# One 512-column pass for both parts of the activations, and PSUM banks handed out in pairs

## The chip, the cores and the metric

The kernel runs on one core of one Trainium2 chip. The metric is the device time of one execution in microseconds (us), as the median of several executions. Engines are named as in the profile: PE is the matrix engine, PEld its weight loads, DVE the vector engine, ACT the activation engine, POOL the general engine, SP the engine that issues most DMA transfers. PSUM is the memory that PE writes its results to; the kernel divides it into eight banks of 512 fp32 columns. "Evacuating" a bank means that ACT or DVE reads the finished result out of it.

## What is computed

Two transformer-like blocks on 256 tokens of width 1024, in fp32. Cut to what matters here:

```
h = rms_norm(x);  q,k,v,rq,rk,rv,rg,ga,gr = split(h @ w_in)
merged = sigmoid(ga) * (att @ w_att_o) + sigmoid(gr) * (ret @ w_ret_o)      # gate, merge
x = x + merged @ w_out
h = rms_norm(x)
x = x + (silu(h @ w_gate) * (h @ w_up)) @ w_down                            # feed-forward
x = second_block(rms_norm(x)):  gated MLP and banded attention, @ w_out, then
x = x + sum over the chosen experts of  g * gelu(expert_u . h) * expert_v   # 16384 experts
```

The expert layer is computed densely: `peer_u` has 128 slices of 128 experts, whose scores for all 256 tokens go through gelu and are multiplied by a sparse matrix of weights, and a second layer multiplies by `peer_v`.

## The kernel before

**Products in two parts.** Every fp32 operand of a large product is split into a high part of type fp32r and a low part, the rest. A product is then three matmuls per k step of 128 rows (`mm3`, L108): weights' high part with activations' high part, high with low, and low with high. Weights are streamed: `unit` (L77) loads 128x1024 values with one SP DMA into `raw`, ACT copies them to `whi` (L95), and DVE subtracts to `wlo` (L96). Six pairs of `whi` and `wlo` are there until the expert layer, three in it.

**Stages.** `gemm_t` (L117) runs 8 k steps of 256 columns (all tokens) into half of one PSUM bank; `gemm_n` (L139) turns the operands round and fills two banks of 128 tokens x 512 columns. In order of time: the q, k, v products (`dests`, L268), attention and retention, gate (L327 to L335, 16 x `gemm_t`), merge (L337 to L350), w_out (L354), the feed-forward layer's gate and up products (L376, 22 values of f) and w_down (L412), block 2 (`block2`, L528) with five `gemm_n` or `gemm_t` groups, and the expert layer (`peer`, L717): 16 query products (L955), 128 slices of the first layer (L994), then the second layer (L1064). Between slices of the first layer the sparse weights are formed and combined (`combine`, L931).

**PSUM.** `mm_bank` (L102) hands out one bank of four in turn, `ax_bank` (L105) one of four others for small products, transposes and the second layer. Before a bank is written again, PE waits for the evacuation of what was in it four `mm_bank` calls ago. The second query and first-layer slices use `mm_bank` too: two slices of 256 columns fill a bank, and ACT puts 512 columns through gelu (L1009; from the time `combine` runs, L1006 and L1009).

**Order.** The order on each engine is set by a scheduler at build time: each engine works off its instructions in that order, and waits on counters of the other engines. `unit` is run 80 places ahead (`AHEAD`).

**Norms.** A norm's per-token factor is made late: column sums by PE (L188), a reciprocal square root by small DVE instructions (L160 to L173), a row form by ACT and PE (L198 to L201). In the feed-forward layer the factor `R` multiplies gate and up (L397 to L401). At the start of block 2 the factor `rd` (L542) scales the q product's evacuation (`qraw`, L557).

Of the kernel before, what the change touches and what calls it, by code (L numbers as in the profile page):

```python
# [7 lines left out]
F32 = mybir.dt.float32  # L8
F32R = mybir.dt.float32r
# [3 lines left out]
AF = mybir.ActivationFunctionType  # L13
OP = mybir.AluOpType
# [14 lines left out]
T = 256  # L29
# [3 lines left out]
KF = FF // 128  # L33
# [8 lines left out]


class Net:
# [36 lines left out]
    def unit_(self, src, n, pieces, engine, between):  # L81
# [18 lines left out]
        return hi, lo  # L100

    def mm_bank(self):  # L102
        return self.psum.tile([128, 512], F32, name="mm", bufs=4)

# [3 lines left out]
    def mm3(self, ps, left, right, first, last):  # L108
        mm = self.nc.tensor.matmul
        mm(ps, lhsT=left[0], rhs=right[0], start=first, stop=False)  # L110
        mm(ps, lhsT=left[0], rhs=right[1], start=False, stop=False)  # L111
        mm(ps, lhsT=left[1], rhs=right[0], start=False, stop=last)  # L112

    def acts(self, hl, k, ts=slice(0, T)):
# [94 lines left out]
    def new_acts(self, pool, K=8, tag="act", bufs=2):  # L209
        return (pool.tile([128, K, T], F32R, tag=tag + "h", name=tag + "h", bufs=bufs),  # L210
                pool.tile([128, K, T], F32R, tag=tag + "l", name=tag + "l", bufs=bufs))

# [22 lines left out]
    def block1(self, actp):  # L235
        nc, a, tc = self.nc, self.a, self.tc
        mult, add, sub = OP.mult, OP.add, OP.subtract
        with ExitStack():
# [6 lines left out]
            first = self.unit_(a["w_in_a"][0], 1024, 4, nc.gpsimd, load_x)  # L245
            h = self.new_acts(actp)
# [13 lines left out]
            with ExitStack() as s1:  # L260
# [42 lines left out]
                both = self.xbp.tile([128, 8, T], F32R, tag="xbh", name="att", bufs=1)  # L303
                att = both[:, 0:4], both[:, 4:8]
                probs = [self.att1_probs(p, tb, aq, ak, mask) for tb in range(2)]
# [21 lines left out]
                for i in range(16):  # L327
                    ps = self.mm_bank()[:, :T]
                    self.gemm_t(ps, a["w_in_a"][14 + i], h, 8)
                    nc.vector.tensor_tensor(out=gate[:, i], in0=ps, in1=R, op=mult)  # L330
                    if i == 2:
                        self.turn_ret(osb, ret)
                    if i % 4 == 3:
                        g4 = gate[:, i - 3:i + 1].rearrange("p a b -> p (a b)")
                        nc.scalar.activation(g4, g4, AF.Sigmoid)  # L335
                mer = self.new_acts(actp)
                for m in range(8):  # L337
                    if m % 2 == 0:
                        hi, lo = self.unit(a["w_att_o"][m // 2], 1024)
                    ps = self.mm_bank()  # L340
                    for k in range(4):
                        s = slice((m % 2 * 4 + k) * 128, (m % 2 * 4 + k) * 128 + 128)
                        self.mm3(ps[:, :T], (hi[:, s], lo[:, s]), self.acts(att, k), k == 0, k == 3)
                    self.gemm_t(ps[:, T:], a["w_ret_o"][m], ret, 8)
                    m1 = p2.tile([128, T], F32, name="m1")
                    m2 = p2.tile([128, T], F32, name="m2")
                    nc.vector.tensor_tensor(out=m1, in0=ps[:, :T], in1=gate[:, m], op=mult)
                    nc.vector.tensor_tensor(out=m2, in0=ps[:, T:], in1=gate[:, 8 + m], op=mult)
                    nc.vector.tensor_tensor(out=m1, in0=m1, in1=m2, op=add)
                    self.split(m1, mer[0][:, m], mer[1][:, m])  # L350
# [15 lines left out]
            with ExitStack() as s1:  # L366
# [9 lines left out]
                for f in range(KF):  # L376
                    ps = self.mm_bank()
                    if f == 0:
# [4 lines left out]
                        continue  # L383
                    self.gemm_t(ps[:, :T], a["w_gate"][f], h, 8)
                    if f == 2:
                        R = self.rows(r, "rb")
                    self.gemm_t(ps[:, T:], a["w_up"][f], h, 8)
                    early.append((ps.rearrange("p (a t) -> p a t", a=2), None))
                    if 5 <= f < 21:
# [4 lines left out]
                    for f0, (g, u) in enumerate(early, f + 1 - len(early)):  # L394
                        gu = p2.tile([128, 2, T], F32, name="gu")
                        if f0:
                            nc.vector.tensor_tensor(out=gu, in0=g, in1=R[:, None, :].to_broadcast([128, 2, T]),  # L397
                                                    op=mult)
                        else:
                            nc.vector.tensor_tensor(out=gu[:, 0], in0=g, in1=R, op=mult)  # L400
                            nc.vector.tensor_tensor(out=gu[:, 1], in0=u, in1=R, op=mult)  # L401
                        nc.scalar.activation(gu[:, 0], gu[:, 0], AF.Silu)
                        nc.vector.tensor_tensor(out=gu[:, 1], in0=gu[:, 0], in1=gu[:, 1], op=mult)
                        self.split(gu[:, 1], hid[0][:, f0], hid[1][:, f0])
                    early = []
# [311 lines left out]
    def peer(self, st, x3, h, acc):  # L717
        nc, a, tc = self.nc, self.a, self.tc
        mult, add, sub = OP.mult, OP.add, OP.subtract
        with tc.using_default_side("right"):  # L720
# [5 lines left out]
            pick = p.tile([128, 3, 128], F32, name="pick")  # L726
        xb = self.new_acts(self.xbp, tag="xb", bufs=1)
        hand = self.pool("hand", 2, st)
# [456 lines left out]
```

## Time and profile before

| | us |
|---|---|
| median of 3 runs | 1287.78 (1287.43 to 1288.07) |
| profiled execution | 1289.19, of which span 1287.4 |
| PE busy | 1276.2 (99%) |
| DVE busy | 904.6 (70%) |
| ACT busy | 718.7 (56%) |

The profile shows one execution. Its span runs from the first to the last instruction of the core; the rest of the execution's time, 1.8 us, lies around it. A matmul's end is modelled, so that neighbouring matmuls overlap in the rows: the time of a matmul in a stream is read from the distance of two starts.

### The profile page before, as it was taken

How to read it: one execution, taken by the hardware profiler on the slowest of the kernel's cores; microseconds unless marked ns; L12 is line 12 of the kernel's file. 1: busy time of each engine (PE TensorE's matmuls, PEld its weight loads, DVE VectorE, ACT ScalarE, POOL GpSimd, SP SyncE). 2: the span in 40 equal slices, each digit the busy share in tenths (PEclk: the TensorE clock that was granted, in tenths of full speed). 3: DMA queues.
4: the chain of work that ended last, by engine and by line, in shares of the span. 5: the costliest groups of instructions: out<-in, count | busy, mean ns of one | idle time of the engine just before them, and what ended most of it. 6: DMA issues, size and time to landing. Idle time of an engine off the chain costs nothing.

```text
span 1287.4 us, 23568 instructions
## 1 busy us (share of the span) xinstructions
PE 1276.2 (99%) x9125; PEld 1186.8 (92%) x9125; DVE 904.6 (70%) x1785; ACT 718.7 (56%) x1158; POOL 269.4 (21%) x173
## 2 busy tenths in 40 slices
PE   8999999999999999999999999999999999999998
PEld 7878999999999889999999999999988888888887
DVE  7767677766666886988895566776566666666665
ACT  5455545545455675655554676666555555555553
POOL 2000000000000000008778887773000000000000
PEclk9999999999999999999999999999999999999999
DMA  7745668965567544567777777776677777777764
GB/s 261 230 131 153 179 188 293 335 195 184 177 186 221 160 145 138 182 187 186 181 168 209 181 169 177 165 172 173 215 217 221 217 215 218 219 219 220 215 199 160
DMA packets 90928, 253.02 MB, mean 197 GB/s; under 512 B 26944, under 2 KB 28736, under 8 KB 90688
## 3 DMA queue, kind: packets, MB, share of 16 engines
q1 hardware_dynamic: 68816, 241.45, 61.0%
q0 software_dynamic: 20992, 8.46, 5.9%
q8 instruction: 71, 1.16, 0.4%
q10 hardware_dynamic: 1008, 1.61, 0.3%
q14 instruction: 41, 0.34, 0.1%
HBM read 240.93 MB, written 10.55 MB: 195 GB/s over the span
## 4 chain that ended last, share of the span: by engine, by line
PE 93%; DVE 5%; issue 1%; DMA 0%; ACT 0%; SPq 0%; ACTq 0%; DVEq 0%
PE ax L1069 27%; PE mm L110 21%; PE mm L112 20%; PE mm L111 20%; DVE wlo L96 2%; PE ax L942 1%; DVE itop L741 1%; PE ax L888 0%; DMA xT<-in_xT_dram 0%; DVE stop L739 0%; ACT whi L95 0%; DVE sc L744 0%; DVE pos L741 0%; PE ax L678 0%; PE ax L713 0%
## 5 line engine op out<-in xcount | busy, mean ns | idle before, releaser
L96 DVE TENSOR_TENSOR wlo<-raw,whi 128x1024 fp32r<-128x1024 f32 (+2 forms) x433 | 524.4, 1213 | 239.6 <-ACT whi L95 238.2
L95 ACT ACTIVATE whi<-raw 128x1024 fp32r<-128x1024 f32 (+3 forms) x439 | 457.9, 1045 | 313.2 <-PE mm L111 219.6
L110 PE MATMUL mm<-xbh,whi 128*128 128x256 f32 x1104 | 312.0, 283 | 0.0
L112 PE MATMUL mm<-xbh,wlo 128*128 128x256 f32 x1104 | 308.3, 279 | 0.3 <-DVE wlo L96 0.2
L111 PE MATMUL mm<-xbl,whi 128*128 128x256 f32 x1104 | 308.3, 279 | 0.2 <-DVE xbl L155 0.2
L832 POOL DMA_INDIRECT cmat<-best,pos x128 | 241.6, 1887 | 226.4 <-DVE itop L741 164.6
L110 PE MATMUL mm<-acth,whi 128*128 128x256 f32 x848 | 239.4, 282 | 3.0 <-DVE qkv L291 1.4
L111 PE MATMUL mm<-actl,whi 128*128 128x256 f32 x848 | 237.9, 281 | 1.5 <-DVE actl L253 1.5
L112 PE MATMUL mm<-acth,wlo 128*128 128x256 f32 x848 | 237.0, 280 | 0.0
L112 PEld LDWEIGHTS mm<-xbh,wlo 128*128 128x128 f32 x1104 | 207.4, 188 | 1.3 <-DVE wlo L96 0.9
L111 PEld LDWEIGHTS mm<-xbl,whi 128*128 128x128 f32 x1104 | 207.6, 188 | 0.4 <-DVE xbl L155 0.4
L110 PEld LDWEIGHTS mm<-xbh,whi 128*128 128x128 f32 x1104 | 207.6, 188 | 0.2 <-ACT xbh L154 0.2
L110 PEld LDWEIGHTS mm<-acth,whi 128*128 128x128 f32 x848 | 159.9, 189 | 4.3 <-DVE qkv L291 1.7
L111 PEld LDWEIGHTS mm<-actl,whi 128*128 128x128 f32 x848 | 160.1, 189 | 2.2 <-DVE actl L253 2.2
L112 PEld LDWEIGHTS mm<-acth,wlo 128*128 128x128 f32 x848 | 160.0, 189 | 0.2 <-DVE wlo L96 0.2
L1069 PE MATMUL ax<-whi,q 128*128 128x512 f32 x512 | 158.0, 389 | 0.0
L1069 PE MATMUL ax<-whi,keys 128*128 128x512 f32 x512 | 157.9, 389 | 0.0
L1069 PE MATMUL ax<-wlo,keys 128*128 128x512 f32 x512 | 157.9, 389 | 0.0
L154 ACT ACTIVATE keys<-S 128x256 fp32r<-128x256 f32 x128 | 53.5, 418 | 151.4 <-PE ax L1069 151.4
L1069 PEld LDWEIGHTS ax<-whi,q 128*128 128x128 f32 x512 | 96.1, 188 | 20.0
L1069 PEld LDWEIGHTS ax<-wlo,keys 128*128 128x128 f32 x512 | 96.1, 188 | 19.9
L1069 PEld LDWEIGHTS ax<-whi,keys 128*128 128x128 f32 x512 | 96.0, 188 | 20.0
(282 smaller groups left out, 1405.5 us busy)
## 6 DMA issues: line engine op xcount, KB each, us to landing
raw<-in_peer_u_dram SPq DMA_DIRECT2D x128, 512.0 KB
raw<-in_peer_v_dram SPq DMA_DIRECT2D x128, 512.0 KB
raw<-in_w_in_b_dram SPq DMA_DIRECT2D x32, 512.0 KB
raw<-in_w_in_a_dram SPq DMA_DIRECT2D x31, 512.0 KB
raw<-in_w_gate_dram SPq DMA_DIRECT2D x22, 512.0 KB
raw<-in_w_up_dram SPq DMA_DIRECT2D x22, 512.0 KB
raw<-in_w_out_dram SPq DMA_DIRECT2D x16, 512.0 KB
cmat<-zero SPq DMA_DIRECT2D x16, 512.0 KB
```

Of the source, the lines that this page charges most:

```text
L95: self.last_copy = nc.scalar.activation(hi[:, s], raw[:, s], AF.Copy).ins
L96: low = (engine or nc.vector).tensor_tensor(out=lo[:, s], in0=raw[:, s], in1=hi[:, s].bitcast(F32), op=OP.subtract)
L110: mm(ps, lhsT=left[0], rhs=right[0], start=first, stop=False)
L111: mm(ps, lhsT=left[0], rhs=right[1], start=False, stop=False)
L112: mm(ps, lhsT=left[1], rhs=right[0], start=False, stop=last)
L154: nc.scalar.activation(hi, src, AF.Copy)
L741: yield cost + 50, lambda: nc.vector.max_index(where[:, o:o + 8], top[:, o:o + 8], vals)
L832: i = nc.gpsimd.indirect_dma_start(self.cmat, bass.IndirectOffsetOnAxis(ap=ps[:, hd, 1, k:k + 1], axis=0), bs[:, hd, 1, k:k + 1], None, co ...
L942: nc.tensor.matmul(C[:, t * 128:t * 128 + 128], lhsT=A[:, t], rhs=G[i][:, t], start=i == 0, stop=i == 1)
L1069: nc.tensor.matmul(banks[tb][d], lhsT=s[left][:, ts], rhs=w[right][:, d * 512:d * 512 + 512], start=first, stop=end)
```

## The change

Where the weights are the stationary operand, the weights' high part meets both parts of the activations in one matmul of 512 columns: high and low part of one k lie side by side in one tile (`new_acts`), the result is high x high in columns 0 to 255 of a bank and high x low in 256 to 511, and the third matmul (low x high) adds to the first 256 columns (`mm2`). The two column halves are added behind it: ACT copies the second, DVE adds (`added`). This is done for gate, merge, the feed-forward gate and up products (f from 1 to 20) and w_down: 720 k steps. Query and expert products keep `mm3`.

PSUM is handed out anew: `mm_pair` is a tile of two banks with two buffers, in place of four single banks, and `mm_bank` gives the first and then the second bank of such a pair to every other product. `R` no longer multiplies the up product; it multiplies behind w_down.

```diff
-    def mm_bank(self):
-        return self.psum.tile([128, 512], F32, name="mm", bufs=4)
+    def mm_pair(self):
+        self.half = None
+        return self.psum.tile([128, 2, 512], F32, name="mm", bufs=2)
+
+    def mm_bank(self):
+        if self.half is None:
+            pair = self.mm_pair()
+            self.half = pair[:, 1]
+            return pair[:, 0]
+        bank, self.half = self.half, None
+        return bank
+    def mm2(self, ps, weight, acts, k, first, last):
+        mm = self.nc.tensor.matmul
+        both = acts[2][:, k]
+        mm(ps, lhsT=weight[0], rhs=both, start=first, stop=False)
+        mm(ps[:, :T], lhsT=weight[1], rhs=both[:, 0], start=False, stop=last)
+    def added(self, out, pair):
+        self.nc.scalar.activation(out, pair[:, :, T:], AF.Copy)
+        self.nc.vector.tensor_tensor(out=out, in0=pair[:, :, :T], in1=out, op=OP.add)
...
                 for i in range(16):
-                    ps = self.mm_bank()[:, :T]
-                    self.gemm_t(ps, a["w_in_a"][14 + i], h, 8)
-                    nc.vector.tensor_tensor(out=gate[:, i], in0=ps, in1=R, op=mult)
+                    if i % 2 == 0:
+                        pair = self.mm_pair()
+                    self.gemm_w(pair[:, i % 2], a["w_in_a"][14 + i], h, 8)
+                    if i % 2:
+                        two = gate[:, i - 1:i + 1]
+                        self.added(two, pair)
+                        nc.vector.tensor_tensor(out=two, in0=two, in1=R[:, None, :].to_broadcast([128, 2, T]),
+                                                op=mult)
...
                 for f in range(KF):
-                    ps = self.mm_bank()
+                    if 0 < f < KF - 1:
+                        pair = self.mm_pair()
+                        self.gemm_w(pair[:, 0], a["w_gate"][f], h, 8)
...
+                        self.gemm_w(pair[:, 1], a["w_up"][f], h, 8)
+                        gu = p2.tile([128, 2, T], F32, name="gu")
+                        self.added(gu, pair)
+                        early.append((gu[:, 0], gu[:, 1]))
+                    else:
+                        ps = self.mm_bank()
...
                 for m in range(8):
-                    ps = self.mm_bank()[:, :T]
+                    ps = self.mm_bank()
                     for j, (k0, K) in enumerate(((0, 8), (8, 8), (16, 6))):
-                        self.gemm_t(ps, a["w_down"][m, :, k0 * 128:(k0 + K) * 128], hid, K, k0, j == 0, j == 2)
-                    nc.vector.tensor_tensor(out=x2[:, m], in0=ps, in1=x1[:, m], op=add)
+                        self.gemm_w(ps, a["w_down"][m, :, k0 * 128:(k0 + K) * 128], hid, K, k0, j == 0, j == 2)
+                    y = p2.tile([128, T], F32, name="y")
+                    nc.scalar.activation(y, ps[:, T:], AF.Copy)
+                    nc.vector.tensor_tensor(out=y, in0=ps[:, :T], in1=y, op=add)
+                    nc.vector.tensor_tensor(out=y, in0=y, in1=R, op=mult)
+                    nc.vector.tensor_tensor(out=x2[:, m], in0=y, in1=x1[:, m], op=add)
```

The order of instructions moves at three places of which the next sections speak. Line numbers here are those of each kernel's own program: L130 to L132 after are `mm3` (L110 to L112 before), L106 and L107 are `whi` and `wlo` (L95, L96), L227 the column sums (L188), L238 the row form (L199), L610 the scaling of q (L557), L1063 the gelu (L1009). Words in brackets say on which engine's counter an instruction waits.

**PE in the first expert layer**, where one bank is full and the next begins. `mm_8557` and `mm_8632` are two banks of before:

```order
L110 MATMUL mm_8557<-xbh_5895,whi_8595 128x256
L111 MATMUL mm_8557<-xbl_5896,whi_8595 128x256
L112 MATMUL mm_8557<-xbh_5895,wlo_8596 128x256
L110 MATMUL mm_8632<-xbh_5895,whi_8634 128x256 [waits Activation_49]
L111 MATMUL mm_8632<-xbl_5896,whi_8634 128x256
L112 MATMUL mm_8632<-xbh_5895,wlo_8635 128x256 [waits DVE_49]
```

After, `mm_8246` is one pair: `whi_8329` belongs to the end of its first bank and `whi_8373` to the start of its second; `mm_8455` is the next pair.

```order
L132 MATMUL mm_8246<-xb_5230,wlo_8330 128x256
L130 MATMUL mm_8455<-xb_5229,whi_8457 128x256 [waits Activation_49]
L131 MATMUL mm_8455<-xb_5229,whi_8457 128x256
L130 MATMUL mm_8246<-xb_5229,whi_8373 128x256 [waits Activation_49]
L131 MATMUL mm_8246<-xb_5229,whi_8373 128x256
L132 MATMUL mm_8246<-xb_5229,wlo_8374 128x256 [waits DVE_49]
```

Two matmuls of the next pair now stand between the first and the second bank of one pair, and the second bank's first matmul carries a wait on ACT of its own, though its weights are two units older than those just used.

**ACT at the same place**, before and after:

```order
L95 ACTIVATE whi_8711<-raw_8710 128x1024 [waits DMAHW3_49,DVE_49,PE_49]
L1009 ACTIVATE S_6234<-mm_8557 128x512 [waits PE_49]
L95 ACTIVATE whi_8752<-raw_8751 128x1024 [waits DMAHW4_49,DVE_49,PE_49]
L95 ACTIVATE whi_8790<-raw_8789 128x1024 [waits DMAHW5_49,DVE_49,PE_49]
L1009 ACTIVATE S_6234<-mm_8632 128x512 [waits PE_49]
```

```order
L106 ACTIVATE whi_8403<-raw_8402 128x1024 [waits DMAHW4_49,DVE_49,PE_49]
L106 ACTIVATE whi_8457<-raw_8456 128x1024 [waits DMAHW5_49,DVE_49,PE_49]
L1063 ACTIVATE S_5565<-mm_8246 128x512 [waits PE_49]
L106 ACTIVATE whi_8487<-raw_8486 128x1024 [waits DMAHW6_49,DVE_49,PE_49]
L106 ACTIVATE whi_8543<-raw_8542 128x1024 [waits DMAHW7_49,DVE_49,PE_49]
L1063 ACTIVATE S_5565<-mm_8246 128x512 [waits PE_49]
```

ACT's order is the same in kind: one gelu of a bank behind every second weight copy, with one copy right ahead of it; both gelus of after read one pair. Counted along ACT's instructions, the counter value for which the first matmul with `whi_8373` waits is that of the first of these gelus.

**PE at the start of block 2.** The q product's two banks are `mm_4764` and `mm_4765` before, and the k product begins in `mm_4919`:

```order
L112 MATMUL mm_4765<-whi_4821,actl_4005 128x512
L188 MATMUL ax_4839<-ones_66,acc_4006 128x1 [waits DVE_49]
L188 MATMUL ax_4839<-ones_66,acc_4006 128x1
L188 MATMUL ax_4857<-ones_66,acg_4007 128x1 [waits DVE_49]
L188 MATMUL ax_4857<-ones_66,acg_4007 128x1
L110 MATMUL mm_4919<-whi_4922,acth_4004 128x512
```

After, q lies in the second bank of `mm_4026` (the first holds w_down's last column block) and in the first of `mm_4110`, and k begins in `mm_4264`, which has the buffer of `mm_4026`:

```order
L132 MATMUL mm_4110<-whi_4166,act_3499 128x512
L227 MATMUL ax_4184<-ones_66,acc_3500 128x1 [waits DVE_49]
L227 MATMUL ax_4184<-ones_66,acc_3500 128x1
L227 MATMUL ax_4202<-ones_66,acg_3501 128x1 [waits DVE_49]
L227 MATMUL ax_4202<-ones_66,acg_3501 128x1
L238 MATMUL ax_4439<-dg_4440,ones_66 128x128 [waits Activation_49]
L238 MATMUL ax_4439<-dg_4443,ones_66 128x128 [waits Activation_49]
L130 MATMUL mm_4264<-whi_4266,act_3499 128x512 [waits PE_49,Activation_49]
```

Of ACT's order after, what precedes and what releases that matmul:

```order
L237 ACTIVATE dg_4440<-ident_139,rcc_4183 128x128 [waits DVE_49]
L237 ACTIVATE dg_4443<-ident_139,rcc_4183 128x128
L240 ACTIVATE rcR_4446<-ax_4439 128x256 [waits PE_49]
L610 ACTIVATE qraw_4236<-mm_4026,rd_4208 128x512 [waits DVE_49,Activation_49]
L610 ACTIVATE qraw_4241<-mm_4110,rd_4208 128x512
```

Before, the first k matmul waits for no other engine's last work here; after, it waits for ACT, and the two row-form products were moved up ahead of it.

## Rows read from the trace of the kernel before

**Rows 1.** Page, part 1: engine, busy us (share of the span), instructions.

```profile
PE 1276.2 (99%) x9125; PEld 1186.8 (92%) x9125; DVE 904.6 (70%) x1785; ACT 718.7 (56%) x1158; POOL 269.4 (21%) x173
```

**Rows 2.** Waits of PE: who waited for what, total us, times, longest; one of eight.

```profile
PE mm L110 <- DVE qkv L291: 1.4, 1, 1.4
```

**Rows 3.** Timeline of the q product: start us, us, engine, line, operation, names.

```profile
418.72 0.40 PE L112 MATMUL mm<-whi,actl 128*128 128x512 f32 x1
418.95 0.40 PE L110 MATMUL mm<-whi,acth 128*128 128x512 f32 x1
419.19 0.40 PE L111 MATMUL mm<-wlo,acth 128*128 128x512 f32 x1
```

**Rows 4.** PE groups, 300 to 400 us: six rows, 852 matmuls; first and last.

```profile
L110 PE MATMUL mm<-hidh,whi 128*128 128x256 f32 x153 | 43.0, 281 | 0.0
...
L112 PE MATMUL mm<-acth,wlo 128*128 128x256 f32 x132 | 36.7, 278 | 0.0
```

**Rows 5.** PE groups, 950 to 1250 us: three rows, 1325 matmuls; the first.

```profile
L1069 PE MATMUL ax<-whi,keys 128*128 128x512 f32 x442 | 136.1, 389 | 0.0
```

**Rows 6.** Timeline where a first-layer bank is full (699.67 is its last matmul).

```profile
699.67 0.28 PE L112 MATMUL mm<-xbh,wlo 128*128 128x256 f32 x1
...
699.78 0.28 PE L110 MATMUL mm<-xbh,whi 128*128 128x256 f32 x1
...
699.87 1.06 ACT L95 ACTIVATE whi<-raw 128x1024 fp32r<-128x1024 f32 x1 [1.74 <-PE mm L111]
...
700.84 0.58 ACT L1009 ACTIVATE S<-mm 128x512 f32<-128x512 f32 x1
```

**Rows 7.** Timeline of PE's longest single wait for an evacuation.

```profile
28.46 0.28 PE L112 MATMUL mm<-acth,wlo 128*128 128x256 f32 x1
...
29.71 1.08 DVE L291 SCALAR_TENSOR_TENSOR qkv<-mm,ra 128x256 f32<-128x256 f32 x3
...
30.19 0.39 PE L110 MATMUL mm<-acth,whi 128*128 128x256 f32 x1 [1.45 <-DVE qkv L291]
...
30.41 0.28 PE L111 MATMUL mm<-actl,whi 128*128 128x256 f32 x1
```

**Rows 8.** Timeline of a full bank while `combine` runs (875.84 its last matmul).

```profile
875.84 0.27 PE L112 MATMUL mm<-xbh,wlo 128*128 128x256 f32 x1
...
875.96 0.62 PE L942 MATMUL ax<-G,A 128*128 128x128 f16 x8
...
877.28 0.42 ACT L1009 ACTIVATE S<-mm 128x304 f32<-128x304 f32 x1
```

**Rows 9.** Timeline of a query product's evacuation (606.69 its last matmul).

```profile
606.69 0.28 PE L112 MATMUL mm<-xbh,wlo 128*128 128x256 f32 x1
...
607.86 0.36 ACT L969 ACTIVATE qT<-mm 128x256 f32<-128x256 f32 x1
```

**Rows 10.** Timeline from the q product's end to its evacuation.

```profile
419.65 0.50 PE L188 MATMUL ax<-ones,acc 128*128 128x1 f32 x4
...
420.46 0.48 PE L110 MATMUL mm<-whi,acth 128*128 128x512 f32 x1
...
424.68 1.23 DVE L96 TENSOR_TENSOR wlo<-raw,whi 128x1024 fp32r<-128x1024 f32 x1 [0.28 <-ACT whi L95]
425.82 0.16 DVE L168 TENSOR_SCALAR rd<-ns 128x2 int32<-128x2 int32 x1
...
428.99 0.69 ACT L557 ACTIVATE qraw<-mm,rd 128x512 f32<-128x512 f32 x1 [1.54 <-DVE rd L542]
```

**Rows 11.** Timeline of the feed-forward norm: column sums and the factor's use.

```profile
226.72 0.50 PE L188 MATMUL ax<-ones,acc 128*128 128x1 f32 x4
...
232.69 0.70 ACT L198 ACTIVATE dg<-ident,rbc 128x128 f32<-128x128 f32 x2 [1.57 <-DVE rbc L173]
```

**Rows 12.** Windows: stretch, us, busy per engine, PEclk (granted clock), DMA share, GB/s.

```profile
8.00:11.00 3.00, 1.56 (x10) 1.36 (x11) 2.60 (x7) 2.15 (x7) 1.40 (x3) 0.97 1.05 362
11.00:14.00 3.00, 2.70 (x13) 2.40 (x13) 3.00 (x7) 2.27 (x5) 0.55 (x1) 0.50 0.97 357
```

More of the change, by code (lines that the diff above doesn't have):

```diff
@@ L41, with __init__, __getitem__ @@
 NSMALL = _o
+class Halves:
+    def __init__(self, parts):
+        self.parts = parts
+    def __getitem__(self, at):
+        return self.parts[at[1] // 4][(at[0], at[1] % 4, *at[2:])]
 class Net:
@@ L100, in unit_ @@
         return hi, lo
+    def mm_pair(self):
+        self.half = None
+        return self.psum.tile([128, 2, 512], F32, name="mm", bufs=2)
     def mm_bank(self):
-        return self.psum.tile([128, 512], F32, name="mm", bufs=4)
+        if self.half is None:
[4 more added lines that the diff above has]
+        return bank
     def ax_bank(self, dt=F32):
@@ L112, in mm3, with gemm_w @@
         mm(ps, lhsT=left[1], rhs=right[0], start=False, stop=last)
+    def mm2(self, ps, weight, acts, k, first, last):
[3 more added lines that the diff above has]
+        mm(ps[:, :T], lhsT=weight[1], rhs=both[:, 0], start=False, stop=last)
+    def gemm_w(self, ps, src, hl, K, k0=0, first=True, last=True):
+        hi, lo = self.unit(src, K * 128)
+        for k in range(K):
+            s = slice(k * 128, k * 128 + 128)
+            self.mm2(ps, (hi[:, s], lo[:, s]), hl, k0 + k, first and k == 0, last and k == K - 1)
+    def added(self, out, pair):
+        self.nc.scalar.activation(out, pair[:, :, T:], AF.Copy)
+        self.nc.vector.tensor_tensor(out=out, in0=pair[:, :, :T], in1=out, op=OP.add)
     def acts(self, hl, k, ts=slice(0, T)):
@@ L209, in new_acts @@
     def new_acts(self, pool, K=8, tag="act", bufs=2):
-        return (pool.tile([128, K, T], F32R, tag=tag + "h", name=tag + "h", bufs=bufs),
-                pool.tile([128, K, T], F32R, tag=tag + "l", name=tag + "l", bufs=bufs))
+        both = pool.tile([128, K, 2, T], F32R, tag=tag, name=tag, bufs=bufs)
+        return both[:, :, 0], both[:, :, 1], both
     def load_const(self, pool, name, shape):
@@ L339, in block1 @@
                         hi, lo = self.unit(a["w_att_o"][m // 2], 1024)
-                    ps = self.mm_bank()
+                    pair = self.mm_pair()
                     for k in range(4):
                         s = slice((m % 2 * 4 + k) * 128, (m % 2 * 4 + k) * 128 + 128)
[L343 to L349, printed above, removed]
+                        self.mm2(pair[:, 0], (hi[:, s], lo[:, s]), att, k, k == 0, k == 3)
+                    self.gemm_w(pair[:, 1], a["w_ret_o"][m], ret, 8)
+                    both = p2.tile([128, 2, T], F32, name="m1")
+                    self.added(both, pair)
+                    nc.vector.tensor_tensor(out=both, in0=both, in1=gate[:, m:16:8], op=mult)
+                    m1 = both[:, 0]
+                    nc.vector.tensor_tensor(out=m1, in0=m1, in1=both[:, 1], op=add)
                     self.split(m1, mer[0][:, m], mer[1][:, m])
@@ L376, in block1 @@
                 for f in range(KF):
-                    ps = self.mm_bank()
+                    if 0 < f < KF - 1:
+                        pair = self.mm_pair()
+                        self.gemm_w(pair[:, 0], a["w_gate"][f], h, 8)
+                        if f == 2:
+                            R = self.rows(r, "rb")
+                        self.gemm_w(pair[:, 1], a["w_up"][f], h, 8)
[4 more added lines that the diff above has]
+                        ps = self.mm_bank()
                     if f == 0:
@@ L383, in block1 @@
                         continue
[L384 to L388, printed above, removed]
+                    if f == KF - 1:
+                        self.gemm_t(ps[:, :T], a["w_gate"][f], h, 8)
+                        self.gemm_t(ps[:, T:], a["w_up"][f], h, 8)
+                        early.append((ps[:, :T], ps[:, T:]))
                     if 5 <= f < 21:
@@ L394, in block1 @@
                     for f0, (g, u) in enumerate(early, f + 1 - len(early)):
[L395 to L404, printed above, removed]
+                        y = p2.tile([128, T], F32, name="y")
+                        nc.vector.tensor_tensor(out=y, in0=g, in1=R, op=mult)
+                        nc.scalar.activation(y, y, AF.Silu)
+                        nc.vector.tensor_tensor(out=y, in0=y, in1=u, op=mult)
+                        self.split(y, hid[0][:, f0], hid[1][:, f0])
                     early = []
@@ L726, in peer @@
             pick = p.tile([128, 3, 128], F32, name="pick")
-        xb = self.new_acts(self.xbp, tag="xb", bufs=1)
+        parts = [self.xbp.tile([128, 4, 2, T], F32R, tag=t, name="xb", bufs=1) for t in ("xbl", "xbh")]
+        xb = [Halves([x[:, :, i] for x in parts]) for i in range(2)] + [Halves(parts)]
         hand = self.pool("hand", 2, st)
```

4 lines of the change are left out of this document (3 added, 1 removed).

## The prediction

> **What bounds the kernel now.** I read the engine shares first: PE is busy 99% of the span [rows 1], so only what shortens PE's work or makes PE wait counts. Next the waits of PE: the list has eight entries, of at most 1.5 us each in total; the longest single wait is 1.4 us, for an evacuation of the q product [rows 2]. The four single banks thus hide every other evacuation. Third the distance of matmul starts, since a shorter PE stream can be read only there. Last, at each place where the order shows a new wait of PE, how long the thing waited for takes in the trace of before. Durations are those of the profiled execution, 1289.19 us, which lies 1.4 us above the median of 1287.78; I make the sum against it and take the 1.4 us off at the end.
>
> **The columns of the pass: about nothing.** A k step had three matmuls of 256 columns; it now has one of 512 and one of 256, again 768 columns. Where two operands of 256 columns follow each other, starts lie 0.117 us apart (699.67 to 699.78 in [rows 6], and 852 matmuls in 100 us, 117.4 ns each, in feed-forward [rows 4]). A 512-column matmul into one bank costs twice that: 418.72, 418.95, 419.19 [rows 3], 0.233 us. So a step takes 3 x 0.1167 = 0.350 before and 0.233 + 0.117 = 0.350 after. In feed-forward, where 117.4 was read, at most 3 x 0.7 = 2 ns a step could go, 1 us over its 496 steps. The best bound is the pace of the second layer, 300 us / 1325 = 226.4 ns per 512 columns [rows 5], where two banks alternate: 339.6 a step, 720 x 10.4 ns = 7.5 us. I take 0.5 us, because the q product, one bank at a time as here, is the nearer row.
>
> The saving that one matmul fewer could bring is what the Trainium skill speaks of ("TensorE: Matmul & The Clock Gate", Back-to-back issue gap): a warm matmul costs its columns at 2.4 GHz and about 2.5 ns fixed, which would make 720 x 2.5 ns = 1.8 us, as an estimate from that page. The rows disagree: 512 columns cost just twice 256, so the fixed part does not show here.
>
> **The added evacuation work: hidden.** ACT's copies and DVE's additions are more, but ACT and DVE are at 56% and 70%, and a pair of banks is written for 4.2 (12 steps) to 5.6 us (16 steps) while the one before is evacuated. Merge and w_out, where DVE is fullest, and the four pairs of w_out and w_down, go into the small terms.
>
> **The pair of banks: new waits of PE.** The order shows what the diff does not: in a pair, the second bank's first matmul waits until the first bank has been read. Before, PE went on to another bank 0.11 us after a bank was full, while gelu still read the old one (699.78 against 700.84, [rows 6]). Now in the expert layer it does two matmuls of the next pair, sometimes more, and stands.
>
> *Price of one.* The bank's last matmul starts at 699.67, PE's next slot is 699.78. ACT first makes the weight copy that PE's progress releases at the same time (699.87, 1.06 us) and then the gelu, 700.84 + 0.58 = 701.42 [rows 6]. The order after has the same copy ahead of the gelu. From an evacuation's end to PE at full pace: the q evacuation's first part ends at 29.71 + 0.42 = 30.13 (0.42 is its duration as one instruction, of three in 1.08), PE starts 30.19 and its second matmul 30.41, one slot of 0.117 after 30.29, so 0.16 us [rows 7]. Delay from PE's free slot: 701.42 - 699.78 + 0.16 = 1.80 us for gelu; for a query product, 607.86 + 0.36 - 606.81 + 0.16 = 1.57 [rows 9]; while `combine` runs, 877.28 + 0.42 - 875.96 + 0.16 = 1.90 [rows 8]. Less what the order puts between the two banks (0.117 us per 256 columns; eight small products of `combine` 0.45, from 875.96 to 876.39 and its slot, [rows 8]).
>
> *Count.* I went through PE's order in the expert layer: 41 second banks wait so, one per four products of 2.8 us. Seven have over 2.2 us of other products between: nothing. Query evacuations: four with 0.47 us between, 4 x 1.1; three with 1.28, 3 x 0.3. Gelu: eight with two or three matmuls (0.23 to 0.35), 8 x 1.55; two with 0.93, 2 x 0.85; one with 1.5, 0.3; two with 1.13, 2 x 0.65; one with 0.68 during `combine`, 1.2; thirteen with 1.13, 13 x 0.75. Sum 4.4 + 0.9 + 12.4 + 1.7 + 0.3 + 1.3 + 1.2 + 9.75 = 32 us. Bounds: if the weight copy did not stand ahead of the evacuation, each loses up to 0.97 us and about 7 are left; if the two matmuls ahead of the wait give no cover, 35.
>
> *Block 2.* The k product's first bank has the buffer in which q's first half lies, and q is read only when `rd` is there. Before, PE went on with k at 420.46 while the first `qraw` ended at 428.99 + 0.69 = 429.68 [rows 10]. PE's free slot is 419.65; with 0.16 that is 10.2 us, less 0.8 for the column sums that stood there before and 0.4 for the row-form products moved into the gap: 9.0. DVE's order after has one weight subtraction in this chain instead of three: each gives back 1.14 us (424.68 to 425.82), but two 0.4 us instructions come in: 7.3. Bounds 6 and 9. After such a gap the clock matters: the early stretch with PE busy 1.56 of 3 us is followed by 3 us granted 0.50, that is 1.2 GHz [rows 12]; half of 3 us lost is 1.5. Later waits for k, v and the output products, whose banks are now halves too: 2.
>
> *Feed-forward start.* The third pair waits until the second has been added up, and ACT does that behind the row form of the norm. That is ready 232.69 + 0.70 - 226.72 = 6.7 us after the column sums [rows 11], PE needs 5.95 for them and the second pair. With ACT's copy of 512 columns (0.7, as the first `qraw` took [rows 10]), DVE's addition (0.7, the same size) and 0.16, PE would go on at 8.2 instead of 5.95, less 0.4 for the row-form products: 1.8 us. Bounds 1 and 3.
>
> *Small terms.* The first q banks: one more evacuation ahead, 0.4. Merge to w_out, w_down's pairs, the output product of block 2 (its fourth bank can begin only when the first has been read): 3.5 together, 1 to 7.
>
> **Sum.** -0.5 + 32 + 7.3 + 1.5 + 2 + 1.8 + 3.9 = 48 us; 1289.2 + 48 = 1337.2, and against the median 1335.8. Rounded: 1335.
>
> **Rivals.**
> *The halves are independent banks.* If PE may write the second bank while the first is read, no wait arises, the columns alone count: 1287, within 0.2%. For it: they are two banks, and before nothing waits [rows 2]. Against it: the order carries the wait, and the scheduler put two matmuls of the next pair in front of it, which it had no need of otherwise. The Trainium skill ("Perfetto Trace Analysis", Matmuls) has the rule by which this would come: groups that rotate through different banks overlap with evacuation. The trace of before agrees, with PE's next matmul 0.11 us after a full bank [rows 6], but there each bank is a tile of its own.
> *The pass runs at the second layer's pace* and the waits are hidden: -7.5, 1280, faster. It decides if the pass frees the weight load, which PEld shows 92% busy [rows 1]. Against: q's 0.233 us [rows 3].
> *The evacuations come sooner*: ACT, with PE standing, has the weight copy done ahead of the gelu. Expert layer 7 instead of 32: 1310. Against: the copy needs the buffer that the same last matmuls free; from 1300 to 1320.
> *The clock falls in the expert layer*: every wait is followed by a stretch at 1.2 GHz. If eight or so of the 1.5 us waits cost 1.5 us more, 1347; at all 34 some 1386. Against: after the 1.7 us gap at 28.6 [rows 7] starts are 0.12 us apart at once, so the clock stayed.
>
> **How the numbers follow.** The forecast, with the bounds of its terms (1322 to 1345), 0.70; sooner evacuations 0.13; the falling clock 0.09; independent halves 0.05; faster pass 0.03. A time within 0.2% of the median, 2.6 us, cannot be told from no change. Faster: 0.03. Same: 0.05. Slower: 0.92. For eight in ten the range takes the forecast's own bounds, and part of the sooner evacuations below and of the clock above: 1308 to 1348.
>
> **What would show it.** Waits of PE on ACT at the gelu line, some 30 of 0.6 to 1.6 us between about 520 and 935 us; PE idle 7 us at the first k matmul, 1.8 us in the third feed-forward pair; starts 0.233 apart in gate and w_down; the second layer still 1536 x 226.4 ns = 348 us. I am wrong if the list of PE's waits stays as short as before, or if gate's 45 us shrink by over 1 us.

## The result, and the profile after

The changed kernel takes 1339.14 us (1339.08 to 1340.56, 4 runs) against 1287.92 us before: 1.0399 times the time, 95% interval 1.0385 to 1.0414. The prediction was 1335, range 1308 to 1348. The profiled execution of after is 1339.12 us, span 1336.8: 49.4 us more than the 1287.4 of before. The profiled execution of before, 1289.19 us, lay 1.3 us above its median, so the medians differ by 51.2 us and the traces by 49.4.

Page of after, part 1, to set against [rows 1]:

```profile
PE 1296.0 (97%) x8405; PEld 1162.8 (87%) x8405; DVE 924.4 (69%) x1820; ACT 741.8 (55%) x1202; POOL 274.8 (21%) x173
```

PE has 720 matmuls fewer and yet is busy longer, in a span of which it fills 97% instead of 99%. (Part of the longer busy time is the lower clock, below.) DVE and ACT have a little more work and a lower share of the span, so neither of them has become the limit. Time went into waits of PE, and the list of waits, to set against [rows 2], names them:

```profile
PE mm L130 <- ACT whi L106: 13.0, 26, 1.3
PE ax L238 <- ACT dg L237: 4.8, 3, 3.4
PE mm L132 <- DVE wlo L107: 3.2, 3, 1.6
PE mm L130 <- ACT qraw L610: 2.7, 1, 2.7
...
PE ax L901 <- DVE pick L864: 2.4, 1, 2.4
```

The largest entry is one that a reader could take amiss: 26 waits for a weight copy (`whi`, L106), not for a gelu. The timeline of one of them, to set against [rows 6], shows what it is:

```profile
751.68 0.27 PE L132 MATMUL mm<-xb,wlo 128*128 128x256 f32 x1
751.88 1.06 ACT L106 ACTIVATE whi<-raw 128x1024 fp32r<-128x1024 f32 x1 [1.69 <-PE mm L131]
752.84 0.58 ACT L1063 ACTIVATE S<-mm 128x512 f32<-128x512 f32 x1
...
752.99 0.38 PE L130 MATMUL mm<-xb,whi 128*128 128x256 f32 x1 [1.03 <-ACT whi L106]
753.21 0.28 PE L131 MATMUL mm<-xb,whi 128*128 128x256 f32 x1
...
753.48 0.39 PE L130 MATMUL mm<-xb,whi 128*128 128x256 f32 x1
```

At 751.68 the first bank of a pair gets its last matmul. The two matmuls at 752.99 and 753.21 are those of the next pair that the order puts ahead, as the two with `whi_8457` in the order shown above. Their weights are copied at 751.88, when PE frees the buffer, so they wait for that copy; behind them the second bank's first matmul starts at 753.48, 0.06 us after gelu's end at 753.42. PE's free slot was 751.80, and it is back at its pace at 753.6, two matmuls (0.23 us) ahead: the price of 1.8 us less the cover of 0.23 that the prediction worked out. The named releaser is the copy because the wait was split in two by the cover; that the pair is the cause is shown by the experiments.

At block 2's start, to set against [rows 10], the timeline of after reads:

```profile
421.09 0.50 PE L227 MATMUL ax<-ones,acc 128*128 128x1 f32 x4
...
425.46 1.22 PE L238 MATMUL ax<-dg,ones 128*128 128x128 f32 x4 [3.42 <-ACT dg L237]
...
428.38 0.16 DVE L595 TENSOR_TENSOR rd<-rd,rcc 128x2 f32<-128x2 f32 x1
428.64 1.27 ACT L610 ACTIVATE qraw<-mm,rd 128x512 f32<-128x512 f32 x2 [1.53 <-DVE rd L595]
429.38 0.79 PE L130 MATMUL mm<-whi,act 128*128 128x512 f32 x1 [2.69 <-ACT qraw L610]
```

The k product starts 8.3 us after PE's free slot of 421.09 (0.8 us before). What follows runs slowly at first; windows of the same stretch (us, busy PE, PEld, DVE, ACT, POOL, then the granted clock):

```profile
424.00:430.00 6.00, 1.84 (x6) 1.46 (x7) 3.86 (x22) 2.44 (x6) 0.00 (x0) 0.50 0.34 100
430.00:433.00 3.00, 3.00 (x9) 2.32 (x8) 2.33 (x8) 1.52 (x4) 0.00 (x0) 0.50 0.00 0
433.00:436.00 3.00, 3.00 (x12) 2.44 (x11) 0.81 (x4) 1.06 (x1) 0.00 (x0) 0.82 0.02 5
```

After the gap the granted clock is 0.50, which is 1.2 GHz, and it is back at 1.00 from 434.2 us on. There is one more such stretch, in the expert layer. PE stands at 697.80 for 1.0 us and at 700.66 for 2.35 us, the second time for `pick`; then its starts lie 0.21 us apart instead of 0.117 until 703.7, which costs 1.3 us (twelve starts in 2.7 us instead of 1.4). The last line is a window:

```profile
700.66 0.69 PE L901 MATMUL ax<-ident,pick 128*128 128x128 f32 x2 [2.35 <-DVE pick L864]
...
701.36 0.41 PE L131 MATMUL mm<-xb,whi 128*128 128x256 f32 x1
701.57 0.41 PE L132 MATMUL mm<-xb,wlo 128*128 128x256 f32 x1
...
700.00:703.00 3.00, 2.34 (x11) 2.35 (x12) 1.82 (x7) 0.23 (x1) 2.69 (x2) 0.56 0.83 185
```

The starts of the same weight unit in the two traces tell where the 49.4 us arise. The lag of after behind before is:

| at the start of | lag, us | gained or lost since |
|---|---|---|
| the last gate product | 0.9 | +0.9 |
| w_out | 0.5 | -0.4 |
| feed-forward product 2 | 4.2 | +3.7 |
| w_down | 1.8 | -2.4 |
| block 2 | 1.4 | -0.4 |
| block 2's k product, second unit | 11.1 | +9.7 |
| the query products | 14.8 | +3.7 |
| the second layer | 49.4 | +34.6 |
| the end | 49.4 | 0 |

So the pass does gain something, in gate, merge, feed-forward and w_down, and 52 us go elsewhere. The first 0.9 us are not the work of gate: the lag is 1.3 us before gate begins, from the kernel's start, and was not taken apart. Of the 3.7 us up to feed-forward product 2, 1.8 arise in w_out and product 0, and 1.9 at the start of product 2.

### The profile page after: what moved, and what is told of

Read it like the earlier page. It is cut to its first block, busy times and chain, and to the rows that moved or that the text cites. A ratio compares the mean times of both kernels' runs of the same rounds, so it can differ in the third digit from the quotient of the medians.

```text
span 1336.8 us, 22176 instructions
## 1 busy us (share of the span) xinstructions
PE 1296.0 (97%) x8405; PEld 1162.8 (87%) x8405; DVE 924.4 (69%) x1820; ACT 741.8 (55%) x1202; POOL 274.8 (21%) x173
## 3 DMA queue, kind: packets, MB, share of 16 engines
q8 instruction: 65, 1.06, 0.3%
## 5 line engine op out<-in xcount | busy, mean ns | idle before, releaser
L107 DVE TENSOR_TENSOR wlo<-raw,whi 128x1024 fp32r<-128x1024 f32 (+2 forms) x433 | 524.6, 1213 | 267.6 <-ACT whi L106 260.1
L106 ACT ACTIVATE whi<-raw 128x1024 fp32r<-128x1024 f32 (+3 forms) x439 | 457.9, 1046 | 329.8 <-PE mm L131 148.3
L130 PE MATMUL mm<-xb,whi 128*128 128x256 f32 x1104 | 314.7, 286 | 12.7 <-ACT whi L106 11.7
L131 PE MATMUL mm<-xb,whi 128*128 128x256 f32 x1104 | 308.6, 280 | 0.0
L132 PE MATMUL mm<-xb,wlo 128*128 128x256 f32 x1104 | 304.7, 281 | 3.5 <-DVE wlo L107 3.2
L886 POOL DMA_INDIRECT cmat<-best,pos x128 | 246.8, 1928 | 239.2 <-DVE pos L871 176.4
L130 PEld LDWEIGHTS mm<-xb,whi 128*128 128x128 f32 x1104 | 208.1, 189 | 22.6 <-ACT whi L106 17.0
L132 PEld LDWEIGHTS mm<-xb,wlo 128*128 128x128 f32 x1104 | 205.9, 188 | 5.0 <-DVE wlo L107 4.9
L131 PEld LDWEIGHTS mm<-xb,whi 128*128 128x128 f32 x1104 | 208.2, 189 | 0.0
L138 PE MATMUL mm<-act,whi 128*128 128x512 f32 x512 | 178.3, 391 | 0.7 <-DVE gu L151 0.7
L139 PE MATMUL mm<-act,wlo 128*128 128x256 f32 x512 | 144.4, 282 | 0.0
L138 PEld LDWEIGHTS mm<-act,whi 128*128 128x128 f32 x512 | 96.1, 188 | 21.0 <-DVE gu L151 0.9
L130 PE MATMUL mm<-act,whi 128*128 128x256 f32 x336 | 96.9, 292 | 4.9 <-DVE qkv L330 1.5
L131 PE MATMUL mm<-act,whi 128*128 128x256 f32 x336 | 95.6, 286 | 3.1 <-DVE act L292 2.4
L139 PEld LDWEIGHTS mm<-act,wlo 128*128 128x128 f32 x512 | 96.8, 189 | 0.0
```

Source lines behind the costliest of these rows:

```text
L106: self.last_copy = nc.scalar.activation(hi[:, s], raw[:, s], AF.Copy).ins
L107: low = (engine or nc.vector).tensor_tensor(out=lo[:, s], in0=raw[:, s], in1=hi[:, s].bitcast(F32), op=OP.subtract)
L138: mm(ps, lhsT=weight[0], rhs=both, start=first, stop=False)
L139: mm(ps[:, :T], lhsT=weight[1], rhs=both[:, 0], start=False, stop=last)
L886: i = nc.gpsimd.indirect_dma_start(self.cmat, bass.IndirectOffsetOnAxis(ap=ps[:, hd, 1, k:k + 1], axis=0), bs[:, hd, 1, k:k + 1], None, co ...
```

## The experiments

**Theory:** the 512-column pass is worth a few us, and the handing out of banks in pairs costs some 50, because a pair is one tile and its second bank is not written until its first has been read. **Rivals:** the pass or its additions cost the time; the expert layer or block 2 is slow for a reason of its own.

**Single banks with the pass.** `mm_pair` gives two single banks, and the halves are added bank by bank:

```diff
     def mm_pair(self):
-        self.half = None
-        return self.psum.tile([128, 2, 512], F32, name="mm", bufs=2)
+        return [self.mm_bank(), self.mm_bank()]
     def mm_bank(self):
...
+        return self.psum.tile([128, 512], F32, name="mm", bufs=4)
     def added(self, out, pair):
-        self.nc.scalar.activation(out, pair[:, :, T:], AF.Copy)
-        self.nc.vector.tensor_tensor(out=out, in0=pair[:, :, :T], in1=out, op=OP.add)
+        for h, bank in enumerate(pair):
+            self.nc.scalar.activation(out[:, h], bank[:, T:], AF.Copy)
+            self.nc.vector.tensor_tensor(out=out[:, h], in0=bank[:, :T], in1=out[:, h], op=OP.add)
```

> The 512-column pass as changed, but four single banks instead of two pairs; the two halves of a result are added bank by bank (ACT copy and DVE addition of 256 columns each, twice as many). Theory (the pairs cause the loss, the pass itself gains): no waits of PE on evacuations, a step of 512 + 256 columns takes 346.7 ns as in the changed kernel against 350.0 in gate and merge and 353.3 in feed-forward and w_down: 224 x 3.3 ns + 496 x 6.6 ns = 4.0 us less than before: 1284 (1283 to 1286). Rival (the pass and its additions cost, the pairs little): 1310 or more, with PE waiting for the additions in gate and feed-forward.

Measured: 1285.5 us (1283.96 to 1287.32, 10 runs), ratio to before 0.9977 (0.9967 to 0.9986). The pass alone makes the kernel faster, by 0.2%, which is little but clear of noise. Its list of PE's waits is as short as that of before:

```profile
PE ax L233 <- ACT dg L232: 1.9, 2, 1.5
PE mm L125 <- DVE act L287: 1.7, 3, 0.8
PE mm L124 <- DVE qkv L325: 1.5, 1, 1.5
```

No entry for `added` is there, though for a pair ACT and DVE now do two copies and two additions of half the size. The theory holds; the rival falls.

**Before with pairs.** The kernel before, in which only `mm_bank` is the changed one:

```diff
     def mm_bank(self):
-        return self.psum.tile([128, 512], F32, name="mm", bufs=4)
+        if self.half is None:
+            pair = self.psum.tile([128, 2, 512], F32, name="mm", bufs=2)
+            self.half = pair[:, 1]
+            return pair[:, 0]
+        bank, self.half = self.half, None
+        return bank
```

> The kernel before with nothing changed but the banks: every bank is half of a two-bank tile. Three matmuls of 256 columns per step, no 512-column pass. Theory (pairs cause the loss): the expert layer loses the same 34 to 35 us as in the changed kernel, block 2's start about 10 us, and gate, merge and feed-forward, where now each second bank also waits for the first, 0 to 1 us at some 22 places: 1342 (1332 to 1355). Rival (the pass causes the loss): 1288.

Measured: 1339.68 us (1339.46 to 1339.89), ratio 1.0399 (1.0380 to 1.0418), the ratio of the changed kernel. Its waits of PE:

```profile
PE mm L116 <- ACT whi L96: 11.8, 25, 1.1
PE ax L205 <- ACT dg L204: 3.4, 1, 3.4
PE mm L116 <- ACT qraw L563: 3.1, 1, 3.1
```

The same entries, with nearly the same longest waits, and without the pass. The banks alone make the loss. That the ratio is the same to the last digit is partly chance: this version has no gain from the pass, but also does not lose 1.9 us at the start of feed-forward product 2. It lags by 4.7 us at block 2 (the changed kernel by 1.4) and loses 33.2 us in the expert layer (34.6).

**Single banks in the expert layer only.** The pool of pairs is closed before the expert layer and four single banks are opened:

```diff
+            self.mmst.close()
+            self.mmp, self.one = self.pool("psm1", 1, space=PSUM), True
             self.peer(st, x3, h, acc)
```

> The changed kernel, but from the expert layer on four single banks take the place of the two pairs. Theory: block 2 and feed-forward as in the changed kernel, the expert layer's 34.6 us gone: 1339.1 - 34.6 = 1304.5, perhaps 1 us more where the pools change over (1303 to 1307). Rival (the expert layer is slow for another reason, such as the activations lying interleaved or the clock): 1339.

Measured: 1306.96 us (1306.81 to 1307.11), 32.2 us under the changed kernel. The lag at block 2 is as in the changed kernel, 1.5 and then 11.4; it is 17.6 when the query products are half through and stays at 17.5 to the end. Of the waits between 560 and 935 us one is left:

```profile
PE mm L137 <- DVE wlo L110: 0.2, 1, 0.2
```

The time is 2.4 us over the 1304.5 that was expected, and the lag rises by as much, from 15.2 to 17.6, at the start of the expert layer. Two waits make it:

```profile
518.14 0.35 PE L135 MATMUL mm<-act,whi 128*128 128x256 f32 x1 [0.61 <-DVE xT L720]
...
PE ax L243 <- ACT dg L242: 1.2, 1, 1.2
```

The first, at the change of pools, costs 0.8 us. The second is the wait for the norm's row form; it costs 1.5 us, and the changed kernel has it too (1.4 us; 1.1 of the 4.8 for `dg` in its list), so single banks could not have taken it away. The interleaved activations, which the expert layer still reads here, cost nothing that shows.

**Evacuation ahead of the weight copy.** From product 34 of the first expert layer on, the weight copy is queued on ACT behind the gelu of the pair's first bank:

```diff
+            with self.tc.issue_after(self.behind) if self.behind else ExitStack():
-            self.last_copy = nc.scalar.activation(hi[:, s], raw[:, s], AF.Copy).ins
+                self.last_copy = nc.scalar.activation(hi[:, s], raw[:, s], AF.Copy).ins
...
+            self.behind = self.evacs[-2] if j >= 34 and e == 0 else None
             self.gemm_t(pair[:, e * T:e * T + T], a["peer_u"][j], xb, 8)
+            self.behind = None
...
-                nc.scalar.activation(S[:, js, done:], p3[:, :, done:], AF.Gelu_apprx_tanh)
+                self.evacs.append(nc.scalar.activation(S[:, js, done:], p3[:, :, done:], AF.Gelu_apprx_tanh).ins)
```

> The changed kernel with one thing moved: in the first expert layer, from product 34 on, the weight copy that stood ahead of every other gelu on ACT is queued behind that gelu. Theory (the wait is the evacuation's end, with the copy's 1.06 us in it): 24 waits of 24.7 us by my sum shrink to about 12 (delay 0.94 to 1.0 us instead of 1.80 to 1.90, less the 0 to 0.9 us of other products that the order has between the banks): 1326.5 (1323 to 1331). Rival (PE waits for something else, or the copy moved behind makes PE wait for its weights instead): 1339 or more.

Measured: 1325.5 us (1324.47 to 1326.53, 2 runs), 13.6 less than the changed kernel. Timeline of one such place, where the order has nothing between the two banks of a pair:

```profile
759.88 0.28 PE L134 MATMUL mm<-xb,wlo 128*128 128x256 f32 x1
...
760.20 0.60 ACT L1067 ACTIVATE S<-mm 128x512 f32<-128x512 f32 x1 [1.83 <-PE mm L134]
760.69 1.05 ACT L108 ACTIVATE whi<-raw 128x1024 fp32r<-128x1024 f32 x1
...
760.85 0.39 PE L132 MATMUL mm<-xb,whi 128*128 128x256 f32 x1 [0.69 <-ACT S L1067]
```

The gelu comes 0.3 us after the bank's last matmul, the copy behind it, and PE goes on at 760.85, 0.05 us after the gelu's end, while the copy is still being made. PE's free slot was 760.00.

Of the waits in its trace one now bears gelu's name:

```profile
PE mm L132 <- ACT S L1067: 5.9, 8, 1.3
```

So PE waits for the evacuation, and the copy's 1.06 us was part of its price, as the sum had it. A gelu with no copy ahead of it still makes PE wait: the order on ACT sizes the wait and does not make it.

**An even start for block 2.** The half pair that is left over is dropped before the q product:

```diff
+            self.half = None
             raw = {"q_g": self.gemm_n(a["w_in2_b"][0], h)}
```

> The changed kernel with one line more: at the start of block 2 the half pair that is left over is dropped, so that the q product fills a pair of its own and the k product the other pair, whose content (w_down's last column blocks) has long been read. Theory (PE stands at block 2's start because k's first bank shares a buffer with q's first half): the 9.7 us there go, with the stretch at 1.2 GHz behind it; the expert layer's waits fall in other places but sum to about the same (my sum 32 against 32): 1339.1 - 9.7 = 1329.4, the waits of k, v and the output products may move it by 3 (1326 to 1333). Rival (PE waits there for the norm itself): 1339.

Measured: 1325.49 us (1324.82 to 1326.16), 13.7 less than the changed kernel, 0.5 us below the range that was expected (1326 to 1333). Timeline at the same place:

```profile
422.61 0.58 PE L227 MATMUL ax<-ones,acg 128*128 128x1 f32 x4
423.06 0.47 PE L130 MATMUL mm<-whi,act 128*128 128x512 f32 x1
```

The k product follows the column sums at once; the lag is 2.6 us at block 2's start and 2.6 at the second k unit, and the granted clock stays at 1.00. All 9.7 us were due to which bank of which pair q and k fell into. The other 4 us are spread over the output products and the expert layer, where the waits fall at other places; they were not taken apart.

**Pairs only where both banks are read together.** Pairs up to feed-forward product 20, single banks from product 21 on:

```diff
+                    if f == KF - 1:
+                        self.mmst.close()
+                        self.mmp, self.one = self.pool("psm1", 1, space=PSUM), True
                     if 0 < f < KF - 1:
```

> The changed kernel with pairs kept up to the feed-forward product 20, where both banks of a pair are read together, and four single banks from product 21 on. Theory: up to the start of w_down as in the changed kernel (1.8 us behind), w_down gains 1.2 us, then no waits of PE for halves: 1289 (1287.5 to 1291.5). Rival (what follows w_down is slow for another reason than the banks): 1335 or more.

Measured: 1295.33 us (1295.17 to 1295.48), 6 more than expected. The place of the 6 us is the change of pools itself:

```profile
345.14 0.38 PE L135 MATMUL mm<-act,whi 128*128 128x256 f32 x1 [2.89 <-DVE gu L156]
```

The first single bank waits for the last pair's addition, and the lag goes from 1.5 us at the last up product but one to 4.5. Behind the wait comes a stretch at 1.2 GHz, with 0.21 us from start to start (the last line is a window, with the clock of 0.50):

```profile
347.02 0.41 PE L137 MATMUL mm<-act,wlo 128*128 128x256 f32 x1
347.24 0.41 PE L135 MATMUL mm<-act,whi 128*128 128x256 f32 x1
...
346.70:350.00 3.30, 3.30 (x17) 3.30 (x17) 0.42 (x1) 1.08 (x2) 0.00 (x0) 0.50 0.20 79
```

It brings the lag to 6.2 at w_down. From there it only falls, to 5.0 at block 2, and rises by 1.3 in the whole rest. The mechanism was right, the price of handing PSUM over in the middle of a stream, 3.0 us for the wait and 1.7 for the clock, was left out.

**The pass cut in two.** Single banks, the 512-column matmul as two of 256 into the two halves of the bank:

```diff
-        mm(ps, lhsT=weight[0], rhs=both, start=first, stop=False)
+        mm(ps[:, :T], lhsT=weight[0], rhs=both[:, 0], start=first, stop=False)
+        mm(ps[:, T:], lhsT=weight[0], rhs=both[:, 1], start=False, stop=False)
```

> The version with single banks, but the 512-column matmul is cut into two of 256 columns into the two halves of the bank: again three matmuls a step, same columns, same additions behind. Tells why a step takes 346.7 ns and not 350.0 or 353.3. If one matmul fewer is what saves (a fixed part per matmul): 350.0 in gate and merge and 350 to 353.3 in feed-forward, 1285.5 + 2.4 to 4 = 1288 to 1289.5. If it is writing in turn to two halves of the bank: 346.7 or less everywhere, 1285.5 or less.

Measured: 1288.5 us (1286.63 to 1290.13, 8 runs), ratio to before 1.0001 (0.9991 to 1.0011): the gain of the pass is gone. Timeline in feed-forward, of the changed kernel and of this one:

```profile
300.15 0.39 PE L138 MATMUL mm<-act,whi 128*128 128x512 f32 x1
300.37 0.28 PE L139 MATMUL mm<-act,wlo 128*128 128x256 f32 x1
300.49 0.39 PE L138 MATMUL mm<-act,whi 128*128 128x512 f32 x1
```

```profile
300.20 0.28 PE L132 MATMUL mm<-act,whi 128*128 128x256 f32 x1
300.32 0.28 PE L133 MATMUL mm<-act,whi 128*128 128x256 f32 x1
300.43 0.28 PE L134 MATMUL mm<-act,wlo 128*128 128x256 f32 x1
300.55 0.28 PE L132 MATMUL mm<-act,whi 128*128 128x256 f32 x1
```

Over many steps the means are 346.7 ns for 512 + 256 columns (228.3 and 118.3), and 350.0 for three of 256 (116.67 each) both in gate and in feed-forward. One matmul fewer saves 3.3 ns a step, as the first theory of this experiment said.

**Four buffers for the copy of x3.** In the single-bank version the row form of the expert layer's norm was late (the 1.9 us entry above), behind a copy that waited for a transfer:

```diff
-                    xt = hand.tile([128, 512], F32, name="xt")
+                    xt = hand.tile([128, 512], F32, name="xt", bufs=4)
```

> The version with single banks, with four buffers instead of two for the transposed copy of x3 (xt). There ACT stood 2.4 us for a transfer of that copy at the start of the query products, with the norm's row form queued behind it, and PE lost 1.6 us. Theory: those 1.6 us come back: 1283.9 (1283 to 1284.6). Rival (the row form is late for its DVE chain): 1285.5.

Measured: 1284.73 us (1284.06 to 1285.9, 9 runs), just above the range that was expected; ratio to before 0.9975 (0.9965 to 0.9985). The entry for `dg` is gone from the list of waits, and the lead over before stays at 4.8 us from block 2 into the expert layer, where the single-bank version fell from 3.5 to 1.6. So the wait went as the theory had it; in the whole-kernel time the step is 0.8 us, which the two intervals do not tell apart, and the gain of 1.6 us is not shown there.

**The pass in the expert layer too.** On top of that, each of the 128 first-layer products takes one bank and the 512-column pass:

```diff
...
-            self.gemm_t(pair[:, e * T:e * T + T], a["peer_u"][j], xb, 8)
+            ps = self.mm_bank()
+            self.gemm_w(ps, a["peer_u"][j], xb, 8)
+            for out, lo, end in ((gt[:, e, :done] if done else None, 0, done), (S[:, j, done:], done, T)):
+                if end > lo:
+                    nc.scalar.activation(out, ps[:, T + lo:T + end], AF.Copy)
+                    nc.vector.tensor_tensor(out=out, in0=ps[:, lo:end], in1=out, op=add)
```

> The version with single banks and four xt buffers, with the 512-column pass also in the 128 products of the first expert layer (one bank a product, ACT copies the second half, DVE adds, gelu from SBUF). Theory: 1024 more steps at 346.7 ns instead of 350.0 to 353: 3.4 to 6.8 us less, 1284.7 - 3.4 = 1281 or better, if DVE has room. Rival: it has none between 570 and 660 us, where it was busy 80.7 of 94 us before and each product now adds 0.42 us, 0.42 x 34 = 14 us: PE then waits for the low parts of the weights, 1285 to 1292.

Measured: 1279.01 us (1278.7 to 1279.66, 4 runs), ratio to before 0.9932 (0.9915 to 0.9949): faster than both kernels. Its windows from 566 to 660 us, where the rival saw no room, and from 725 to 935 us:

```profile
566.00:660.00 94.00, 93.88 (x597) 84.84 (x596) 89.11 (x331) 57.91 (x91) 70.14 (x37) 1.00 0.73 189
725.00:935.00 210.00, 210.00 (x1362) 183.88 (x1361) 172.74 (x369) 163.85 (x436) 112.31 (x69) 1.00 0.69 182
```

In the first DVE is busy 89.1 of 94 us, and PE is idle for 0.12 us; in the second DVE is busy 172.7 of 210 us and ACT 163.9, and PE is never idle. The additions had room, between 566 and 660 us only just.

## Why the prediction was right

**What binds.** PE at 99% with nothing to spare, so that every new wait of PE is paid in full: the lag table adds up to the whole difference of the two traces, with nothing given back later (the second layer's start and end lag by the same 49.4 us). The cause was right as well as the number: pairs without the pass lose as much, the pass without pairs loses nothing.

**The expert layer.** Predicted 32 us, lag +34.6, and 32.2 less with single banks there. The price of one wait was the step on which most rested; the timeline of after has it to 0.1 us, and moving the copy changed the time by 13.6 where the sum said 12.6. The rival of the sooner evacuations was a true mechanism, but does not come about by itself: the copy is released by the same matmuls. That 32 stands so near 34.6 is partly luck. The sum left out a wait of 2.4 us for the transposes of `pick` (L901), the low clock behind it (1.3), 3.2 us for weights' low parts and 1.4 for the norm's row form, 8.3 us together. That leaves some 26 us for the waits on evacuations that the sum put at 32. For the thirteen gelus at 0.75 the trace agrees, with 0.7 us lost from pair to pair while `combine` runs; which of the other terms were too large was not taken apart.

**Block 2.** Predicted 7.3 and 1.5 for the clock, 8.8; the lag grew by 9.7. The chain was right (its terms as written add up to 7.5, not 7.3): the first `qraw` ends 429.3 in after, 8.2 us behind PE's free slot. The low clock lasted longer than the 3 us that I took from the early stretch: from 424 to 433 at 0.50 and to 436 at 0.82, some 2.3 us of matmul time lost after the k product's start. The products that follow, and the output product: +3.7 against 2 and a share of the small terms.

**Feed-forward start.** Predicted 1.8 for the third pair, where the lag grew by 1.9; and, for merge, w_out, w_down and block 2's output product, 3.5, of which 1.8 show in w_out and product 0.

**The columns: the term that was mis-sized.** I took 0.5 us and gave a best bound of 7.5. Against the trace of before it is about 4: 3.3 ns on 224 steps and 6.6 on 496. Between the medians it is 2.5 (1287.99 for before in that series, 1285.5 with single banks), and 3.3 ns on all 720 steps would be 2.4. The failing step was to read a 512-column matmul's price from the q product [rows 3]: there 233 ns, in the pass 228.3. For the same reason the sign that starts would lie 0.233 us apart in gate and w_down did not come. And I dismissed the Trainium skill's fixed part of about 2.5 ns for a warm matmul ("TensorE: Matmul & The Clock Gate", Back-to-back issue gap), because 512 columns cost twice 256 in those rows; the cut pass shows 3.3 ns for one matmul fewer, so here the page was nearer than the row. The rest against the trace of before, 3.3 ns on the 496 steps of feed-forward and w_down, is that 256-column starts lay 117.8 ns apart in that execution; whether they do in its other executions no trace shows.

**The rivals.** Independent halves: what they would give was right in kind, and the rule that the Trainium skill states ("Perfetto Trace Analysis", Matmuls), that groups rotating through different banks overlap with evacuation, holds in these runs when the banks are tiles of their own, 1285.5 us, and not when two banks are one tile, 1339. The falling clock in the expert layer came once in place of eight times: behind the waits of 1.0 and 2.35 us at 697.80 and 700.66 the clock was low until 703.7 and took 1.3 us. Behind the other waits there, single ones of up to 1.6 us, it stayed at 1.00.

## What to carry to other kernels

What a buffer is for the scheduler is decided by the tile, not by the bank: where one tile held two banks that are filled and read at different times, the second was not written until the first had been read, and the same four banks no longer hid the evacuations. Before a resource that several stages share is cut anew for the sake of one, look at the order of the stages that did not change, at the first write to each buffer and what it waits for. And the name in a list of waits can be that of a cover in front of the real cause: the 26 waits for a weight copy went away when the banks were parted, with a copy still right ahead of the gelu.

## What the runs showed of the hardware

A 512-column matmul in the pass, with the next matmul of 256 columns into the first half of the same bank, takes 228.3 ns and the 256-column one 118.3; 512 columns behind 512 in the q product take 233.4; alternating between two banks in the second layer 226.7. A 256-column stream runs at 116.67 ns in one stretch and at 117.78 in another of the same form and in these traces stays so until something interrupts it (before: gate the one, feed-forward the other; with the cut pass, feed-forward 116.67). What sets the one or the other was not found; it is worth 1.7 us over this kernel's 496 steps.
